# Decode loads and cache copies of a hybrid decoder layer issued from GpSimd's queue instead of SyncE's

## The chip, the cores and the metric

The kernel runs on one core of a Trainium2 chip. The metric is the time of one execution on the device in microseconds (us). The engines are TensorE (PE, with its weight loads as PEld), VectorE (DVE), ScalarE (ACT), GpSimd (POOL) and SyncE (SP); each works through its own instructions in order, and they meet at semaphores. SP does nothing here but issue DMAs. GpSimd computes a little and issues DMAs too. "SPq" and "POOLq" in the profile's rows are the DMA queues of these two.

## The reference

One decoder layer, for a prompt of 1024 tokens and eight samples of one token each that share its weights. The samples' attention to the memory and the two window caches are what the change touches.

```
z = x @ w_in                                  # split into xr, yr, q, k, v, xq and three gates
xc, conv_new = causal_conv(xr, conv_buf, conv_w, conv_b)     # conv_new: the last 3 rows of [conv_buf, xr]
hs, h_new = rg_lru(xc, h0, ...)
a_out = hs * gelu(yr)
s_out, wk_new, wv_new = swa_decode(q, k, v, win_k, win_v, sinks)   # wk_new = [win_k, k][-128:]
c_out = mem_attn(xq, mem_k, mem_v)            # softmax(xq . mem_k / 16) @ mem_v, 4 heads of 256, 256 rows
merged = sum(sigmoid(g_n + b_n) * (br_n @ w_branch[n]) for the three branches)
h = layer_norm(ALPHA * x + merged @ w_out)
h = layer_norm(ALPHA * h + (silu(gt) * up) @ w_down)
```

All inputs and outputs are float32; `mem_k` and `mem_v` hold 8 x 256 x 4 x 256 numbers each, the two window caches 8 x 128 x 256 each.

## The kernel before, in words

Every matrix product is done in three float32r products of a high and a low part: ACT casts the high part (`split`, L81), DVE subtracts the low one (L82), PE multiplies three times (L115 to L117, L300 to L302, L1178 to L1180). The big projections are done in units of two column tiles by a fast scheme of seven products, the quarters 0 to 6. A unit loads four halves of weights (`half_raw`, L92, tile `ur`) into six rotating buffers; quarters 1, 2, 4 and 5 are sums of them (L284, tile `us`), and three quarters are prepared ahead of PE.

The stages follow one another: the opening and the projection of z (`project`), memory attention and windows with the branch products as filling, the output projection, the gate-and-up products in units (`units`), and the down product. In the projection two side jobs are pumped along, a step every quarter or two: the recurrent branch `lru`, and for each head h the decode attention to the memory, `dec_mem(h)`. PE's accumulation banks are emptied by ACT (`p1s`, `p5s`, `u2s`, and `zb` at L1393) and DVE (`za`, `zb` at L327 to L332), and each bank has to be empty before PE writes it again.

`dec_mem(h)` writes the eight queries of the head to the memory outside, and for each pair of samples reads them back spread over all partitions (L809, tile `dcq`, two buffers). For each of the eight samples it loads 256 KB of keys (L811, tile `dck`, two buffers), and DVE forms two sums of products with them (L815, tile `dcj`). After a softmax the same is done with the probabilities (L833, `dcpb`) and the values (L835, `dcv`; L839, `dcw`). Over the four heads that is 32 loads of keys, 32 of values and 32 spread ones, all on SP's queue, between the projection's weight loads and the stores of its results.

In `lru`, GpSimd copies what has to be kept of the convolution's state: two rows of the samples' old state (L741, one copy for each of eight channel tiles m), the new row (L742) and the prompt's last three (L740). It also computes one step of the recurrence (L768, tile `tr`) and keeps the last state (L775, L776). GpSimd's queue further carries the loads of two thirds of branch a's rows (L136, tiles H) and of the down product's rows (L1253, `gl`).

In `units` the two window caches are copied from input to output, shifted by one row, 1016 KB each: at unit 6 keys (`o_swk`), at unit 12 values (`o_swv`), at L1226 on SP's queue, behind the last weight load issued so far. Results of a unit are stored from `ft` to `scr_f` by two stores on SP (L1204).

The order in which each engine takes its instructions is not the order of the code: a scheduler sets it by priorities and by its own estimates of when things will be ready. `issue_after(ins)` puts what its block issues behind `ins` on the engine of `ins`.

Of the kernel before, what the change touches and what calls it, by code (L numbers as in the profile page):

```python
# [10 lines left out]
F32 = mybir.dt.float32  # L11
# [7 lines left out]
P = 128  # L19
# [39 lines left out]
class Builder:  # L59
# [645 lines left out]
    def lru_setup(self):  # L705
        self.scv = self.cst.tile([P, KT, 3, NB], F32, name="scv")
        self.scvo = self.cst.tile([P, KT, 3, NB], F32, name="scvo")
        self.sh = self.cst.tile([P, KT, NB], F32, name="sh")
        self.sho = self.cst.tile([P, KT, NB], F32, name="sho")
        self.pconv = self.cst.tile([P, KT, 3], F32, name="pconv")  # L710
        self.pho = self.cst.tile([P, KT], F32, name="pho")

    def load_lru(self):
        self.nc.sync.dma_start(self.scv, self.io["scv"])
        self.nc.sync.dma_start(self.sh, self.io["sh"])

    def store_lru(self):
        nc, io = self.nc, self.io
# [5 lines left out]
    def lru(self, m, xr, yr):  # L724

        nc, io, vec = self.nc, self.io, self.vec
        col = lambda base: vec[:, base + m:base + m + 1]
        stt = nc.vector.scalar_tensor_tensor
        wr = self.z.tile([P, 256], F32, tag="wlr", name=f"wlr{m}", bufs=1)
        nc.sync.dma_start(wr, io["wlru"][m])  # L730
        cw = [col(V_CW + 8 * i) for i in range(4)]
        xc = self.zt(f"xc{m}")
        nc.scalar.activation(xc, xr, AF.Identity, bias=col(V_CB), scale=cw[3])
        buf = self.scv[:, m, :, :]
        for i in (2, 1, 0):
            d = 3 - i
            stt(xc[:, d:TP], xr[:, :TP - d], cw[i], xc[:, d:TP], op0=ALU.mult, op1=ALU.add)
            stt(xc[:, TP:T], buf[:, i, :], cw[i], xc[:, TP:T], op0=ALU.mult, op1=ALU.add)
            yield
        nc.gpsimd.tensor_copy(self.pconv[:, m, :], xr[:, TP - 3:TP])  # L740
        nc.gpsimd.tensor_copy(self.scvo[:, m, 0:2, :], buf[:, 1:3, :])  # L741
        nc.gpsimd.tensor_copy(self.scvo[:, m, 2, :], xr[:, TP:T])  # L742
        wgh, wgl = (self.z.tile([P, 256], F32R, tag=f"wg{e}", name=f"wg{e}{m}", bufs=1) for e in "hl")
        self.split(wgh, wgl, wr)
        a, ti = self.zt(f"tr{m}"), self.zt(f"ti{m}")
        for c, (t0, n) in enumerate(THIRDS):
            xch, xcl = (self.z.tile([P, n], F32R, tag=f"xc{e}", name=f"xc{e}{m}_{c}", bufs=1) for e in "hl")
            self.split(xch, xcl, xc[:, t0:t0 + n])
            yield
            for j, (dst, hb) in enumerate(((a, self.hba), (ti, self.hbx))):  # L750
                ps = self.bank("o", f"g{m}_{j}_{c}")[:, :n]
                self.mm3(ps, [((wgh[:, j * P:(j + 1) * P], wgl[:, j * P:(j + 1) * P]), (xch, xcl))])
                nc.scalar.activation(dst[:, t0:t0 + n], ps, AF.Tanh, bias=hb[:, m:m + 1], scale=0.5)
                yield

        sp2, sp4n = self.sp2[:, m:m + 1], self.sp4n[:, m:m + 1]
        stt(ti, ti, 1.0, xc, op0=ALU.add, op1=ALU.mult)
        th = self.zt(f"th{m}")
        nc.scalar.activation(th, a, AF.Tanh, bias=sp2, scale=sp2)
        yield  # L760
        nc.scalar.activation(a, a, AF.Exp, bias=sp4n, scale=sp4n)
        yield
        sq = self.zt(f"sq{m}")
        nc.scalar.activation(sq, th, AF.Sqrt)
        stt(th, a, 1.0, th, op0=ALU.add, op1=ALU.mult)
# [10 lines left out]
        nc.gpsimd.tensor_copy(self.sho[:, m, :], sq[:, TP:T])  # L776
# [23 lines left out]
    def dec_mem(self, h):  # L800
# [5 lines left out]
        for b in range(NB):  # L806
            if b % 2 == 0:
                qb = ph.tile([P, 512], F32, tag="dq", name=f"dcq{b}_{h}", bufs=2)
                nc.sync.dma_start(qb.rearrange("p (b d) -> p b d", b=2), qr[b:b + 2, :].partition_broadcast(P))  # L809
            kk = ph.tile([P, 512], F32, tag="dk", name=f"dck{b}_{h}", bufs=2)  # L810
            nc.sync.dma_start(kk.rearrange("p (t d) -> p t d", t=2),  # L811
                              io["cmk"][b, :, h * 256:(h + 1) * 256].rearrange("(t p) d -> p t d", p=P))
            for kt in range(2):
                junk = ph.tile([P, 256], F32, tag="dj", name=f"dcj{b}_{h}_{kt}", bufs=1)
                nc.vector.scalar_tensor_tensor(junk, kk[:, kt * 256:(kt + 1) * 256], 1.0,  # L815
                                               qb[:, (b % 2) * 256:(b % 2 + 1) * 256], op0=ALU.mult, op1=ALU.mult,
                                               accum_out=sc[:, kt, b:b + 1])
            yield
# [11 lines left out]
        for b in range(NB):  # L830
            if b % 2 == 0:
                pb = ph.tile([P, 512], F32, tag="dq", name=f"dcpb{b}_{h}", bufs=2)
                nc.sync.dma_start(pb.rearrange("p (b k) -> p b k", b=2), pd[b:b + 2, :].partition_broadcast(P))  # L833
            vv = ph.tile([P, 512], F32, tag="dk", name=f"dcv{b}_{h}", bufs=2)
            nc.sync.dma_start(vv.rearrange("p (f k) -> p f k", f=2),  # L835
                              io["cmvT"][b, h * 256:(h + 1) * 256, :].rearrange("(f p) k -> p f k", p=P))
            for f in range(2):
                junk = ph.tile([P, 256], F32, tag="dj", name=f"dcw{b}_{h}_{f}", bufs=1)
                nc.vector.scalar_tensor_tensor(junk, vv[:, f * 256:(f + 1) * 256], 1.0,  # L839
# [366 lines left out]
    def units(self):  # L1206
# [13 lines left out]
        for n, (f, i) in enumerate(todo):  # L1220
            if i == 1 and f + 1 < NF:
                load(f + 1)
            if (f, i) in ((6, 2), (12, 2)):
                name, cache = ("o_swk", "cwk") if f == 6 else ("o_swv", "cwv")
                with self.tc.issue_after(self.last_load):
                    self.nc.sync.dma_start(io[name][:, 0:P - 1, :], io[cache][:, 1:P, :])  # L1226
# [294 lines left out]
```

## Time and profile before

| | us |
|---|---|
| median of three runs | 1951.6 (1949.46 to 1952.06) |
| the profiled execution | 1951.06 |
| its span, first to last instruction | 1949.3 |
| mean granted TensorE clock | 0.997 |
| PE waits for other engines, 90 to 600 us | 3.3 |
| PE waits for other engines, 1300 to 1700 us | 2.3 |

The profile is of one execution. A row of the waits names the waiting engine, line and tile, then the engine, line and tile that ended the wait. A row of the timeline gives start, duration, engine, line, operation, output and inputs, and in square brackets how long the engine had been idle and what ended that. Rows with two times and a colon are stretches: length, then the busy time and number of instructions of PE, PEld, DVE, ACT and GpSimd, the granted clock, the share of the DMA engines and GB/s.

### The profile page before, as it was taken

How to read it: one execution, taken by the hardware profiler on the slowest of the kernel's cores; microseconds unless marked ns; L12 is line 12 of the kernel's file. 1: busy time of each engine (PE TensorE's matmuls, PEld its weight loads, DVE VectorE, ACT ScalarE, POOL GpSimd, SP SyncE). 2: the span in 40 equal slices, each digit the busy share in tenths (PEclk: the TensorE clock that was granted, in tenths of full speed). 3: DMA queues.
4: the chain of work that ended last, by engine and by line, in shares of the span. 5: the costliest groups of instructions: out<-in, count | busy, mean ns of one | idle time of the engine just before them, and what ended most of it. 6: DMA issues, size and time to landing. Idle time of an engine off the chain costs nothing. (4 is left out here: it accounts for less than half of the span.)

```text
span 1949.3 us, 37970 instructions
## 1 busy us (share of the span) xinstructions
PE 1912.5 (98%) x14356; PEld 1880.8 (96%) x14356; DVE 1364.0 (70%) x2875; ACT 1013.5 (52%) x2198; POOL 141.9 (7%) x218
## 2 busy tenths in 40 slices
PE   8999999999999999999999999999999999999997
PEld 8999999999999999989999999999999999999997
DVE  8678887888777555379877557976565665757566
ACT  5465565465556445378775245643333333635444
POOL 1000000000011200012210000000000000402002
PEclk9999999999999999999999999999999999999999
DMA  7444545365323866567534341122222222846554
GB/s 231 145 164 147 171 166 183 128 216 168 130 90 137 275 213 206 156 169 221 157 88 154 118 142 44 45 75 99 78 87 88 87 82 71 279 131 190 155 159 139
DMA packets 170919, 281.92 MB, mean 145 GB/s; under 512 B 20864, under 2 KB 85456, under 8 KB 170704
## 3 DMA queue, kind: packets, MB, share of 16 engines
q1 hardware_dynamic: 165840, 264.72, 43.0%
q0 software_dynamic: 4896, 14.78, 2.3%
q8 instruction: 112, 1.84, 0.4%
q14 instruction: 71, 0.58, 0.1%
HBM read 214.64 MB, written 66.85 MB: 144 GB/s over the span
## 5 line engine op out<-in xcount | busy, mean ns | idle before, releaser
L1246 PE MATMUL dl<-gh,wd_l 128*128 128x384 f32 (+1 forms) x528 | 167.4, 317 | 3.0 <-DVE wd_l L82 3.0
L1244 PE MATMUL dl<-gh,wd_h 128*128 128x384 f32 (+1 forms) x528 | 167.0, 317 | 1.0 <-ACT gh L81 1.0
L1245 PE MATMUL dl<-gl,wd_h 128*128 128x384 f32 (+1 forms) x528 | 167.2, 317 | 0.0
L1246 PEld LDWEIGHTS dl<-gh,wd_l 128*128 128x128 f32 x528 | 99.0, 188 | 3.5 <-DVE wd_l L82 3.5
L1244 PEld LDWEIGHTS dl<-gh,wd_h 128*128 128x128 f32 x528 | 98.9, 188 | 1.3 <-ACT gh L81 1.3
L1245 PEld LDWEIGHTS dl<-gl,wd_h 128*128 128x128 f32 x528 | 99.0, 188 | 0.5 <-DVE gl L82 0.5
L1253 POOL DMA_DIRECT2D gl<-scr_f x66 | 35.6, 540 | 789.0 <-PE fb L1179 630.8
L81 ACT CAST u_1h<-us 128x512 fp32r<-128x512 f32 x48 | 29.8, 621 | 87.6 <-issue 43.5
L592 ACT ACTIVATE bp<-bp,bst 128x257 f32<-128x257 f32 (+1 forms) x128 | 62.8, 493 | 18.0 <-DVE bst L588 17.7
L284 DVE TENSOR_TENSOR us<-ur,ur 128x512 f32<-128x512 f32 x96 | 66.0, 688 | 5.0 <-DMA ur<-win 2.9
L81 ACT CAST u_2h<-us 128x512 fp32r<-128x512 f32 x48 | 29.7, 619 | 76.5 <-PE fb L1179 38.2
L284 DVE TENSOR_TENSOR us<-us,ur 128x512 f32<-128x512 f32 x96 | 66.2, 689 | 2.3
L82 DVE TENSOR_TENSOR u_6l<-ur,u_6h 128x512 fp32r<-128x512 f32 x48 | 33.0, 688 | 43.8 <-PE fb L1180 28.5
L115 PE MATMUL brs<-bsH,wbs_h 128*128 128x384 f32 (+1 forms) x192 | 61.0, 319 | 1.0 <-ACT bsH L81 1.0
L82 DVE TENSOR_TENSOR u_4l<-us,u_4h 128x512 fp32r<-128x512 f32 x48 | 33.0, 687 | 40.1 <-PE fb L1180 29.1
L116 PE MATMUL brs<-bsL,wbs_h 128*128 128x384 f32 (+1 forms) x192 | 61.0, 318 | 0.0
L117 PE MATMUL brs<-bsH,wbs_l 128*128 128x384 f32 (+1 forms) x192 | 60.9, 317 | 0.0
L588 DVE CUSTOM_DVE_ANT_0 bp<-bs,mask,nsnk 128x256 f32<-128x256 f32 (+1 forms) x128 | 54.7, 458 | 3.3 <-PE bs L585 2.2
L82 DVE TENSOR_TENSOR u_5l<-us,u_5h 128x512 fp32r<-128x512 f32 x48 | 33.1, 690 | 30.0 <-PE fd L1180 14.6
L1198 ACT ACTIVATE ft<-za 128x516 f32<-128x516 f32 x40 | 25.5, 636 | 52.4 <-DVE za L1197 52.0
L81 ACT CAST u_5h<-us 128x512 fp32r<-128x512 f32 x48 | 30.0, 625 | 38.2 <-DVE us L284 24.7
L81 ACT CAST u_0h<-ur 128x512 fp32r<-128x512 f32 x48 | 29.8, 621 | 38.1 <-PE ub L301 19.2
(2019 smaller groups left out, 8112.7 us busy)
## 6 DMA issues: line engine op xcount, KB each, us to landing
ur<-win SPq DMA_DIRECT2D x112, 256.0 KB
ur<-wgu SPq DMA_DIRECT2D x80, 256.0 KB
scr_f<-ft SPq DMA_DIRECT2D x40, 258.0 KB
gl<-scr_f POOLq DMA_DIRECT2D x44, 192.0 KB, 4.8
dck<-cmk SPq DMA_DIRECT2D x32, 256.0 KB
dcv<-cmvT SPq DMA_DIRECT2D x32, 256.0 KB
st<-scr_q SPq DMA_DIRECT2D x32, 256.0 KB
scr_g<-za SPq DMA_DIRECT2D x10, 516.0 KB
```

The source lines that it names most:

```text
L81: ins = self.nc.scalar.copy(hi, src).ins
L82: self.nc.vector.tensor_sub(lo, src, hi.bitcast(F32))
L115: nc.tensor.matmul(ps, sh, mh, start=i == 0, stop=False)
L116: nc.tensor.matmul(ps, sh, ml, start=False, stop=False)
L117: self.last_mm = nc.tensor.matmul(ps, sl, mh, start=False, stop=closes and i == last).ins
L284: nc.vector.tensor_add(src, a, b)
L588: nc.vector.tensor_tensor_reduce(pg[g], s[:, u * 256:u * 256 + n], msk, 1.0, snk[:, g:g + 1], ALU.add, ALU.min, st[:, g:g + 1])
L592: nc.scalar.activation(x, x, AF.Exp, bias=st[:, g:g + 1], scale=-1.0, accum_out=st[:, 4 + g:5 + g])
L1244: nc.tensor.matmul(ps, sh, mh, start=k == 0, stop=False)
L1245: nc.tensor.matmul(ps, sh, ml, start=False, stop=False)
L1246: self.last_mm = nc.tensor.matmul(ps, sl, mh, start=False, stop=closes and k == NF - 1).ins
L1253: self.nc.gpsimd.dma_start(lo.bitcast(F32), self.scf[f][:, t0:t0 + n])
```

## The change

It does three things. The 96 loads of `dec_mem` go out from GpSimd's queue, the key loads behind GpSimd's copy of the convolution's old state. That copy is made once, for all eight channel tiles, right after the state is loaded. And the two cache copies go out from GpSimd's queue too, each behind a new tiny copy on GpSimd (`pace`) that reads the first `p1s` tile of its unit.

```diff
@@ load_lru
+        self.conv_kept = self.nc.gpsimd.tensor_copy(self.scvo[:, :, 0:2, :], self.scv[:, :, 1:3, :]).ins
@@ lru
         nc.gpsimd.tensor_copy(self.pconv[:, m, :], xr[:, TP - 3:TP])
-        nc.gpsimd.tensor_copy(self.scvo[:, m, 0:2, :], buf[:, 1:3, :])
         nc.gpsimd.tensor_copy(self.scvo[:, m, 2, :], xr[:, TP:T])
@@ dec_mem, keys
-                nc.sync.dma_start(qb.rearrange("p (b d) -> p b d", b=2), qr[b:b + 2, :].partition_broadcast(P))
+                nc.gpsimd.dma_start(qb.rearrange("p (b d) -> p b d", b=2), qr[b:b + 2, :].partition_broadcast(P))
             kk = ph.tile([P, 512], F32, tag="dk", name=f"dck{b}_{h}", bufs=2)
-            nc.sync.dma_start(kk.rearrange("p (t d) -> p t d", t=2),
-                              io["cmk"][b, :, h * 256:(h + 1) * 256].rearrange("(t p) d -> p t d", p=P))
+            with self.tc.issue_after(self.conv_kept):
+                nc.gpsimd.dma_start(kk.rearrange("p (t d) -> p t d", t=2),
+                                    io["cmk"][b, :, h * 256:(h + 1) * 256].rearrange("(t p) d -> p t d", p=P))
...
@@ dec_mem, values: the loads of pb and vv likewise from nc.sync to nc.gpsimd
...
@@ units
-                with self.tc.issue_after(self.last_load):
-                    self.nc.sync.dma_start(io[name][:, 0:P - 1, :], io[cache][:, 1:P, :])
+                with self.tc.issue_after(self.nc.gpsimd.tensor_copy(self.pace, st[f]["s", 0, 0][:, :1]).ins):
+                    self.nc.gpsimd.dma_start(io[name][:, 0:P - 1, :], io[cache][:, 1:P, :])
```

The scheduler's order changes with it. PE's order differs at two places only, the starts of units 8 and 14, where the two halves' first products were interleaved before and now stand one after the other.

On SP around the first cache copy (`ur` are the weight halves of one unit, `scr_f_85` to `scr_f_87` the results of units 5 to 7), before:

```order
L92 DMA ur_11_17775<-wgu 128x512
L1226 DMA o_swk<-cwk 8x2x16256
L1204 DMA scr_f_85<-ft_0_17613 256x1x258
L1204 DMA scr_f_85<-ft_1_17629 256x1x258
L1204 DMA scr_f_86<-ft_0_17866 256x1x258
L1204 DMA scr_f_86<-ft_1_17882 256x1x258
L92 DMA ur_00_18022<-wgu 128x512
L92 DMA ur_01_18024<-wgu 128x512
L92 DMA ur_10_18026<-wgu 128x512
L92 DMA ur_11_18028<-wgu 128x512
L1204 DMA scr_f_87<-ft_0_18118 256x1x258
L1204 DMA scr_f_87<-ft_1_18134 256x1x258
```

and with the change:

```order
L92 DMA ur_11_17769<-wgu 128x512
L1206 DMA scr_f_85<-ft_0_17607 256x1x258
L1206 DMA scr_f_85<-ft_1_17623 256x1x258
L92 DMA ur_00_18017<-wgu 128x512
L92 DMA ur_01_18019<-wgu 128x512
L92 DMA ur_10_18021<-wgu 128x512
L92 DMA ur_11_18023<-wgu 128x512
L1206 DMA scr_f_86<-ft_0_17861 256x1x258
L1206 DMA scr_f_86<-ft_1_17877 256x1x258
L92 DMA ur_00_18269<-wgu 128x512
L92 DMA ur_01_18271<-wgu 128x512
```

The copy is gone from SP, and each unit's two stores again alternate with the four loads of a later unit; before, the stores of `scr_f_85` and `scr_f_86` stood together ahead of the loads.

On ACT, where unit 8's first quarter is split (`u_0h`) and unit 7's gate is formed (`ft`), before:

```order
L1190 COPY u2s_0_18084<-fb_0_17992 128x258
L1190 COPY u2s_1_18098<-fb_1_18007 128x258
L1198 ACTIVATE ft_0_18118<-za_0_18117 128x516
L1198 ACTIVATE ft_1_18134<-za_1_18133 128x516
L81 CAST u_0h<-ur_00_18022 128x512
L81 CAST u_1h<-us_1_18168 128x512
L81 CAST u_2h<-us_2_18206 128x512
L81 CAST u_3h<-ur_01_18024 128x512
```

and with the change:

```order
L1192 COPY u2s_0_18079<-fb_0_17987 128x258
L81 CAST u_0h<-ur_00_18017 128x512
L1192 COPY u2s_1_18093<-fb_1_18002 128x258
L81 CAST u_1h<-us_1_18163 128x512
L81 CAST u_2h<-us_2_18201 128x512
L1200 ACTIVATE ft_0_18113<-za_0_18112 128x516
L81 CAST u_3h<-ur_01_18019 128x512
L1200 ACTIVATE ft_1_18129<-za_1_18128 128x516
```

The cast of `u_0h` stood behind both tanh of `ft` and now stands ahead of them.

On SP in the key loop of head 1 before (`dcq` the spread queries, `dck` the keys, one row per sample):

```order
L809 DMA dcq_1_2509<-dcq_2501 128x512
L809 DMA dcq_1_2689<-dcq_2501 128x512
L811 DMA dck_1_2691<-cmk 128x2x256
L92 DMA ur_01_2904<-win 128x512
L811 DMA dck_1_2771<-cmk 128x2x256
L809 DMA dcq_1_2857<-dcq_2501 128x512
L811 DMA dck_1_2859<-cmk 128x2x256
L92 DMA ur_10_2906<-win 128x512
L811 DMA dck_1_2948<-cmk 128x2x256
L809 DMA dcq_1_3027<-dcq_2501 128x512
```

and on GpSimd with the change:

```order
L742 COPY pconv<-za_2110 128x3
L743 COPY scvo<-za_2110 128x8
L813 DMA dck_1_2596<-cmk 128x2x256
L810 DMA dcq_1_2509<-dcq_2501 128x512
L810 DMA dcq_1_2689<-dcq_2501 128x512
L813 DMA dck_1_2691<-cmk 128x2x256
L813 DMA dck_1_2771<-cmk 128x2x256
L810 DMA dcq_1_2857<-dcq_2501 128x512
L813 DMA dck_1_2859<-cmk 128x2x256
L813 DMA dck_1_2948<-cmk 128x2x256
```

The same loads in the same order, without weight loads between them, behind GpSimd's own copies of the recurrent branch.

On DVE in the same loop (`dcj` the sums of products, `za` and `zb` the emptying of PE's banks, `u_6l` and `u_0l` weight splits), before:

```order
L815 SCALAR_TENSOR_TENSOR dcj_1_0_2773,dcs_2508<-dck_1_2771,dcq_1_2689 128x256
L815 SCALAR_TENSOR_TENSOR dcj_1_1_2775,dcs_2508<-dck_1_2771,dcq_1_2689 128x256
L327 TENSOR_TENSOR za_2701<-uc_1_2716,p1s_1_2589 128x258
L82 TENSOR_TENSOR u_0l<-ur_00_2602,u_0h 128x512
L815 SCALAR_TENSOR_TENSOR dcj_1_0_2861,dcs_2508<-dck_1_2859,dcq_1_2857 128x256
L815 SCALAR_TENSOR_TENSOR dcj_1_1_2863,dcs_2508<-dck_1_2859,dcq_1_2857 128x256
L329 SCALAR_TENSOR_TENSOR zb_2739<-ub_0_2561,p5s_0_2629 128x258
L815 SCALAR_TENSOR_TENSOR dcj_1_0_2950,dcs_2508<-dck_1_2948,dcq_1_2857 128x256
L815 SCALAR_TENSOR_TENSOR dcj_1_1_2952,dcs_2508<-dck_1_2948,dcq_1_2857 128x256
L329 SCALAR_TENSOR_TENSOR zb_2739<-ub_1_2576,p5s_1_2644 128x258
```

and with the change:

```order
L817 SCALAR_TENSOR_TENSOR dcj_1_0_2861,dcs_2508<-dck_1_2859,dcq_1_2857 128x256
L817 SCALAR_TENSOR_TENSOR dcj_1_1_2863,dcs_2508<-dck_1_2859,dcq_1_2857 128x256
L327 TENSOR_TENSOR za_2701<-uc_1_2716,p1s_1_2589 128x258
L82 TENSOR_TENSOR u_0l<-ur_00_2602,u_0h 128x512
L817 SCALAR_TENSOR_TENSOR dcj_1_0_2950,dcs_2508<-dck_1_2948,dcq_1_2857 128x256
L817 SCALAR_TENSOR_TENSOR dcj_1_1_2952,dcs_2508<-dck_1_2948,dcq_1_2857 128x256
L329 SCALAR_TENSOR_TENSOR zb_2739<-ub_0_2561,p5s_0_2629 128x258
L817 SCALAR_TENSOR_TENSOR dcj_1_0_3031,dcs_2508<-dck_1_3029,dcq_1_3027 128x256
L329 SCALAR_TENSOR_TENSOR zb_2739<-ub_1_2576,p5s_1_2644 128x258
L82 TENSOR_TENSOR u_1l<-us_1_2777,u_1h 128x512
```

The sums of the fifth and sixth sample stand closer together, and a first sum of the seventh (`dck_1_3029`) now stands ahead of the second `zb`; before, it came behind `za`, further down.

More of the change, by code (lines that the diff above doesn't have):

```diff
@@ L710, in lru_setup @@
         self.pconv = self.cst.tile([P, KT, 3], F32, name="pconv")
+        self.pace = self.cst.tile([P, 1], F32, name="pace")
         self.pho = self.cst.tile([P, KT], F32, name="pho")
@@ L832, in dec_mem @@
                 pb = ph.tile([P, 512], F32, tag="dq", name=f"dcpb{b}_{h}", bufs=2)
-                nc.sync.dma_start(pb.rearrange("p (b k) -> p b k", b=2), pd[b:b + 2, :].partition_broadcast(P))
+                nc.gpsimd.dma_start(pb.rearrange("p (b k) -> p b k", b=2), pd[b:b + 2, :].partition_broadcast(P))
             vv = ph.tile([P, 512], F32, tag="dk", name=f"dcv{b}_{h}", bufs=2)
-            nc.sync.dma_start(vv.rearrange("p (f k) -> p f k", f=2),
-                              io["cmvT"][b, h * 256:(h + 1) * 256, :].rearrange("(f p) k -> p f k", p=P))
+            nc.gpsimd.dma_start(vv.rearrange("p (f k) -> p f k", f=2),
+                                io["cmvT"][b, h * 256:(h + 1) * 256, :].rearrange("(f p) k -> p f k", p=P))
             for f in range(2):
```

## The prediction

> **What bounds the kernel now.** I read the page's first two parts, then PE's waits as a whole and by stage, then the stretches in which PE stood still, and last the queues of SP and GpSimd (POOL).
>
> ```profile
> span 1949.3 us, 37970 instructions
> PE 1912.5 (98%) x14356; PEld 1880.8 (96%) x14356; DVE 1364.0 (70%) x2875; ACT 1013.5 (52%) x2198; POOL 141.9 (7%) x218
> ```
>
> PE is busy for 98% of the span, so 1949.3 - 1912.5 = 36.8 us is all that any change of waits could ever return. The moved loads lie in the projection (about 30 to 470 us), the two cache copies in the unit stage (1354 and 1477 us). These are PE's waits between 90 and 600 us, and those between 1300 and 1700 us (line, tile, released by; us in total, times, longest):
>
> ```profile
> PE ub L300 <- ACT zb L1393: 2.0, 2, 1.4
> PE g L115 <- ACT tr L753: 0.5, 1, 0.5
> PE ub L300 <- DVE zb L329: 0.5, 1, 0.5
> PE vt L407 <- DVE v L419: 0.3, 1, 0.3
> ...
> PE fb L1180 <- DVE u_0l L82: 1.3, 2, 0.6
> ```
>
> That is 3.3 us in the projection and 1.3 us in the unit stage: 4.6 us in 1950, or 0.24%. A measurement of this kernel can tell about 0.2%, or 3.9 us, from no change. The ceiling of the gain is therefore just over what can be seen; a loss has no such ceiling.
>
> Why PE waits in the unit stage is seen on SP around the first copy (start, duration, line, DMA, count):
>
> ```profile
> 1337.18 1.19 SPq L1204 DMA_DIRECT2D scr_f<-ft  x2
> 1341.62 12.56 SPq L92 DMA_DIRECT2D ur<-wgu  x4
> 1354.23 0.86 SPq L1226 DMA_DIRECT2D o_swk<-cwk  x1
> 1357.30 21.30 SPq L1204 DMA_DIRECT2D scr_f<-ft  x4
> 1378.69 2.03 SPq L92 DMA_DIRECT2D ur<-wgu  x4
> ```
>
> The normal turn is two stores, then four weight loads. Behind the copy the stores of two units stand together, the second pair waits for its unit to end, and the next unit's loads are issued at 1378.7, some 17 us after their usual time of 1361.7 (1341.6 plus the 20 us of a unit). The order of the work on ACT was made for loads that late: the gate's two tanh stand ahead of u_0h.
>
> ```profile
> 1393.76 0.64 ACT L1198 ACTIVATE ft<-za 128x516 f32<-128x516 f32 x1 [7.33 <-DVE za L1197]
> 1395.74 0.60 ACT L81 CAST u_0h<-ur 128x512 fp32r<-128x512 f32 x1
> 1398.61 0.39 PE L1180 MATMUL fb<-H_0h,u_0l 128*128 128x258 f32 x1 [0.64 <-DVE u_0l L82]
> 1520.21 0.39 PE L1180 MATMUL fb<-H_0h,u_0l 128*128 128x258 f32 x1 [0.64 <-DVE u_0l L82]
> ```
>
> ACT sits idle for 7.3 us in front of a tanh while the loads have landed, u_0h and so u_0l come late, and PE waits 0.64 us; the same again behind the second copy.
>
> In the projection the worst wait is in the key loop of head 1. First DVE's rows, then those behind it:
>
> ```profile
> 187.12 0.43 DVE L815 SCALAR_TENSOR_TENSOR dcj<-dck,dcq 128x256 f32<-128x256 f32 x1 [2.34 <-DMA dcq<-dcq]
> 190.98 0.42 DVE L815 SCALAR_TENSOR_TENSOR dcj<-dck,dcq 128x256 f32<-128x256 f32 x1 [0.64 <-DMA dck<-cmk]
> 199.02 0.43 DVE L815 SCALAR_TENSOR_TENSOR dcj<-dck,dcq 128x256 f32<-128x256 f32 x1 [1.42 <-DMA dck<-cmk]
> 203.32 0.42 DVE L332 TENSOR_TENSOR za<-ud,u2s 128x258 f32<-128x258 f32 x1
> 203.77 0.21 ACT L1412 ACTIVATE qdc<-za 128x8 f32<-128x8 f32 x1 [2.45 <-DVE za L332]
> 204.84 0.37 ACT L1393 ACTIVATE zb<-ub 128x258 f32<-128x258 f32 x1
> 205.25 0.39 PE L300 MATMUL ub<-t01h,u_0h 128*128 128x258 f32 x1 [1.42 <-ACT zb L1393]
> ```
>
> DVE works in order, so its waits for the decode loads push back za, which ACT needs for qdc, behind which stands the zb that frees PE's bank. Here DVE's lateness goes straight into PE. Over the whole projection DVE waits so:
>
> ```profile
> DVE dcj L815 <- DMA dck<-cmk: 7.1, 10, 1.4
> DVE dcw L839 <- DMA dcv<-cmvT: 7.0, 7, 1.7
> DVE dcj L815 <- DMA dcq<-dcq: 4.8, 3, 2.3
> DVE dcw L839 <- DMA dcpb<-dcpd: 2.3, 4, 0.8
> ```
>
> 21.2 us of waits for decode loads cost PE at most its 3.3 us; the rest went into the time in which DVE would have waited for PE anyway.
>
> **The change, part by part.**
>
> *The two cache copies off SP.* In the new order SP's loads and stores keep their normal turn through both places, u_0h stands ahead of both tanh, and PE's two interleaved openings are straight. What is gained is the two waits of 0.64 us: -1.3. The count of matmuls in the stretch says it could be a little more: 36 against 44 in an undisturbed 5 us (the second row below), 8 x 5/44 = 0.9 us; twice that is 1.8, the other end.
>
> ```profile
> 1395.00:1400.00 5.00, 4.36 (x36) 4.15 (x36) 4.87 (x11) 1.77 (x4) 0.00 (x0) 1.00 0.32 105
> 1355.00:1360.00 5.00, 5.00 (x44) 5.00 (x44) 3.54 (x9) 1.63 (x3) 0.00 (x0) 1.00 0.96 319
> ```
>
> The copy itself keeps the DMA engines full for about 5 us (the last row: share 0.96). From GpSimd it starts when the new small copy `pace` has read the unit's first p1s, about 1.5 us into unit 6. Unit 8 starts near 1398 (PE's wait above), unit 6 two units of 20 us earlier, so that is near 1359; there the copy meets the first two weight loads of unit 8 at 1361.7. Those are needed by u_0h near 1386 (20 us after 1365.9, where unit 7's u_0h ran): 24 us of cover, so nothing. `pace` also gives p1s a second reader, on an engine with nothing else to do there: nothing.
>
> *One conv copy instead of eight.* GpSimd saves seven of eight copies, and now the first loads stand behind the one.
>
> ```profile
> 25.60 5.31 POOL L741 COPY scvo<-scv 128x16 f32<-128x16 f32 x8 [25.16 <-DMA scv<-scv]
> 30.50 1.03 SPq L811 DMA_DIRECT2D dck<-cmk  x2
> 83.81 0.42 DVE L815 SCALAR_TENSOR_TENSOR dcj<-dck,dcq 128x256 f32<-128x256 f32 x1 [2.04 <-DMA dcq<-dcq]
> ```
>
> The first two key loads go out at about 27 instead of 30.5 and are used at 83.8: nothing. GpSimd was idle before and after those copies: nothing.
>
> *The 96 decode loads from SP to GpSimd.* Three effects. First, the issue: 96 x 0.54 us = 52 us of GpSimd time in 440 us (twice that, 104, if a load of 256 short rows takes double the 128 rows of gl), on an engine that is 7% busy: no bound. What it holds up are GpSimd's own small steps (pconv, tr, pho, sho); I laid the times of these in the trace against the new order, and none of them stands ahead of a load that was issued earlier than it ran. Second, dcq no longer queues on SP behind stores and weight loads. Third, the time from issue to data, L, may grow, and two buffers per load mean that each pair of batches waits one L.
>
> ```profile
> 182.05 1.42 SPq L809 DMA_DIRECT2D dcq<-dcq  x2
> 188.05 0.38 SPq L811 DMA_DIRECT2D dck<-cmk  x1
> 194.18 0.38 SPq L811 DMA_DIRECT2D dck<-cmk  x1
> ...
> L1253 POOL DMA_DIRECT2D gl<-scr_f x66: 536/538/595, 1662.9 to 1856.4; - x66
> DMA to landing us min/median/max: 2.7/4.3/5.4
> ...
> DMA to landing us min/median/max: 2.6/3.7/4.8
> ```
>
> On SP, L was at most 187.12 - 182.05 = 5.1 us for dcq, 190.98 - 188.05 = 2.9 and 199.02 - 194.18 = 4.8 for dck; a middle of 3.8. From GpSimd no 256 KB load is in the trace; the nearest are gl (192 KB, beside full DMA engines: 2.7/4.3/5.4) and the H rows of the branch stage (192 KB: 2.6/3.7/4.8, the last row). They bound L by 2.6 and 5.4. I take 3.5: a little under the H rows' median because those are sixteen loads issued in a row, well above their minimum because the load is a third larger and has twice as many rows. The new order on DVE puts the pairs nearer together and one pair more ahead of za, so three rounds of L now stand between the first dcj and za. By DVE's rows and L = 3.5 za ends 17.7 us after the first dcj, against 203.32 + 0.34 - 187.12 = 16.5 before: +1.2. The first dcj comes when dcq lands: at 3.5 to 4.3 instead of 5.1 it is 0.8 to 1.6 earlier: -1.2. Sum for this loop: 0. The loop of head 0 is built alike (its PE wait is the other 0.6): 0. The other six loops cost PE 0.5 us at most, and their slack takes up a half us per round. Ends: both zb waits and the 0.5 gone, -2.5; L at 4.3, three rounds in two loops, 6 x 0.8 = +4.8.
>
> The Trainium skill (DMA: Bandwidth & Descriptors, section Latency and other measured facts) gives about 1 us to the first byte for GpSimd's DMAs and 0.6 for SP's. By that estimate L would be 2.9 + 0.4 = 3.3 in an idle machine and the sum 6 x 0.2 = 1.2 us lower than mine; the trace has no pair of equal loads from both queues, so I leave the sum at the rows.
>
> **Sum.** -1.3 (unit stage) + 0 (projection) + 0 (the rest) = -1.3: the profiled execution's 1951.06 (span 1949.3 and 1.8 around it) becomes 1949.8. The median of the three runs is 1951.6, 0.5 higher; on that scale it is 1950.3.
>
> **Rivals.**
>
> *B, the projection gains too.* If SP's queue was what made dcq and dck late, as 4.8 and 5.1 against 2.9 suggest, DVE's waits fall, and PE's waits on ub (2.5) and g (0.5) go with them: -1.8 - 3.0 = -4.8, 1946.8. Against it: the denser order on DVE, and that PE's waits were spread over four causes.
>
> *C, slower: the loads land later from GpSimd.* In the loops of heads 0 and 1 PE's wait follows DVE's one for one, over six rounds. From L = 3.5 + 1.3/6 = 3.7 it eats the gain of the unit stage; at 4.3, gl's median, it is +4.8 - 1.3 = +3.5, and with a half us from each of two other dense loops, +4.5: 1956. For it: the H rows' median is 3.7, and more than half of gl's loads took 4.3. Against it: those were issued one behind another, while here at most four are under way.
>
> *D, slower by far: GpSimd does not get its descriptors out beside a busy DVE.* The worst case in the trace is a tiny GpSimd copy that took 3.5 us instead of 0.2 beside a DVE scan:
>
> ```profile
> L776 POOL COPY sho<-sq x8: 191/394/3545, 152.5 to 618.5; 128x8 f32<-128x8 f32 x8
> L827 DVE TENSOR_SCALAR dcp<-dcp,dcst 8x256 f32<-8x256 f32 x4 | 1.3, 336 | 0.0
> ```
>
> If each of six rounds were held for 3.3 us more, that is +20, 1970. Against it: GpSimd's DMA issues took 595 ns at the longest. The Trainium skill (SBUF - State Buffer, section Who interferes with whom) says that GpSimd's descriptor writing is locked out only by DVE copies, casts and tensor_scalar in a two-port mode, not by tensor_tensor. By that rule D needs such instructions, and the last row shows the only ones between 80 and 470 us: four, 1.3 us in all.
>
> *E, it does nothing:* the copies still disturb PE from their new place, and the loads are hidden anyway: 1951.6.
>
> **How the numbers follow.** Forecast 0.58, B 0.17, C 0.17, D 0.03, E 0.05. The range goes from B's 1946.8 to just under C's 1956 and leaves out D and half of C. Faster by over 0.2% (under 1947.7) is most of B and a sliver of the forecast: 0.18. Slower (over 1955.5) is about two thirds of C, and D: 0.16. Within it: 0.66.
>
> **What would show it.** Right: no PE wait on u_0l after 1300 us; SP's stores and loads in their turn; PE's waits on zb in the first 250 us between 1 and 3.5 us; a landing time of dck between 3 and 4. Wrong: dck and dcv landing at over 4.2 us with PE waiting on zb more often (C), or DVE's waits for decode loads falling under 12 us and PE's zb waits gone (B); GpSimd issues of several us (D).

## The result, and the profile after

| kernel | median of the runs, us | lowest to highest |
|---|---|---|
| before, beside it | 1951.83 (4 runs) | 1949.46 to 1954.84 |
| changed | 1972.63 (4 runs) | 1965.50 to 1975.98 |

The ratio is 1.0111, with a 95% interval of 1.0093 to 1.0129: the change costs some 21 us. The forecast was 1950.3. The profiled execution of the changed kernel is the fastest of its four, 1965.5; the other three had a mean granted clock of 0.991 to 0.993 where this one has 0.995, and that difference is part of the story below.

First the page: the first part, then the DMA issues (KB each, median us from issue to landing).

```profile
span 1963.7 us, 38011 instructions
PE 1916.2 (98%) x14356; PEld 1884.7 (96%) x14356; DVE 1364.4 (69%) x2875; ACT 1013.4 (52%) x2198; POOL 195.9 (10%) x311
...
ur<-win SPq DMA_DIRECT2D x112, 256.0 KB, 3.3
...
dck<-cmk POOLq DMA_DIRECT2D x32, 256.0 KB, 3.8
dcv<-cmvT POOLq DMA_DIRECT2D x32, 256.0 KB, 3.4
```

PE's busy time grew by only 3.7 us, the span by 14.4. GpSimd is busy for 54 us more and far from a bound. The landings lie in the band that the prediction called right, between 3 and 4, and yet the kernel is slower. Where the time goes is seen in PE's waits between 90 and 600 us (us in total, times, longest):

```profile
PE ub L300 <- DVE zb L329: 8.2, 4, 3.2
PE ub L300 <- ACT zb L1395: 4.0, 3, 1.7
PE ub L300 <- ACT zb L1393: 2.4, 2, 2.0
PE g L116 <- DVE xcl L82: 1.3, 2, 0.7
PE g L115 <- ACT tr L754: 0.6, 1, 0.6
PE dct L823 <- ACT vd L409: 0.3, 1, 0.3
```

That is 16.8 us where it was 3.3, and 14.6 of it is PE waiting for a bank that zb has not yet freed. DVE's waits for the decode loads went from 21.2 to 37.0 us:

```profile
DVE dcj L817 <- DMA dck<-cmk: 17.8, 15, 2.0
DVE dcw L841 <- DMA dcv<-cmvT: 10.5, 10, 2.1
DVE dcj L817 <- DMA dcq<-dcq: 4.4, 3, 2.8
DVE dcw L841 <- DMA dcpb<-dcpd: 4.3, 3, 1.9
```

How the one becomes the other is seen in the value loop of head 0, where PE had waited for nothing before. DVE's rows in that stretch, before and then after, are cut to the waits for loads, a weight split (`u_5l`) as a mark of how far DVE has come, and what stands nearest to zb (`ge` and the scan belong to the recurrent branch):

```profile
131.37 0.43 DVE L839 SCALAR_TENSOR_TENSOR dcw<-dcv,dcpb 128x256 f32<-128x256 f32 x1 [0.56 <-DMA dcpb<-dcpd]
...
146.45 0.69 DVE L82 TENSOR_TENSOR u_5l<-us,u_5h 128x512 fp32r<-128x512 f32 x1
...
149.41 2.28 DVE L772 TENSOR_TENSOR_SCAN sq<-tr,ti 128x1024 f32<-128x1024 f32 x1
...
154.56 0.41 DVE L329 SCALAR_TENSOR_TENSOR zb<-ub,p5s 128x258 f32<-128x258 f32 x1
154.90 1.22 DVE L781 SCALAR_TENSOR_TENSOR ge<-ge,zb 128x1032 f32<-128x1032 f32 x1
```

```profile
132.69 0.43 DVE L841 SCALAR_TENSOR_TENSOR dcw<-dcv,dcpb 128x256 f32<-128x256 f32 x1 [1.16 <-DMA dcpb<-dcpd]
...
138.06 0.42 DVE L841 SCALAR_TENSOR_TENSOR dcw<-dcv,dcpb 128x256 f32<-128x256 f32 x1 [0.55 <-DMA dcv<-cmvT]
...
144.33 0.42 DVE L841 SCALAR_TENSOR_TENSOR dcw<-dcv,dcpb 128x256 f32<-128x256 f32 x1 [1.17 <-DMA dcv<-cmvT]
...
149.66 0.69 DVE L82 TENSOR_TENSOR u_5l<-us,u_5h 128x512 fp32r<-128x512 f32 x1
...
156.23 1.23 DVE L782 SCALAR_TENSOR_TENSOR ge<-ge,zb 128x1032 f32<-128x1032 f32 x1
157.38 2.28 DVE L773 TENSOR_TENSOR_SCAN sq<-tr,ti 128x1024 f32<-128x1024 f32 x1
...
159.64 0.42 DVE L329 SCALAR_TENSOR_TENSOR zb<-ub,p5s 128x258 f32<-128x258 f32 x1
```

The first zb comes 5.1 us later than before, and two things add up in that. DVE lost 0.56 us to decode loads before and 2.88 us after; these 2.3 us are most of the 3.2 us by which u_5l is late. Apart from its waits for the loads DVE has no gap of note in this stretch, in either kernel, so it never gets the time back before the next zb. The other 1.9 us come behind u_5l and are the new order: it puts two more sums (0.7 us) and one `ge` (1.2 us), which stood behind this zb before, ahead of it. PE's row behind it, and then the clock (per stretch: length, busy time of PE, PEld, DVE, ACT and GpSimd with counts, granted clock, DMA share, GB/s):

```profile
160.11 0.39 PE L300 MATMUL ub<-ts60h,u_6h 128*128 128x258 f32 x1 [3.17 <-DVE zb L329]
```

```profile
156.00:160.00 4.00, 0.94 (x8) 0.74 (x7) 4.00 (x6) 2.09 (x3) 0.70 (x2) 1.00 0.77 239
...
160.30:163.70 3.40, 3.40 (x17) 3.40 (x17) 3.40 (x7) 0.79 (x1) 0.85 (x2) 0.51 0.02 5
163.70:167.00 3.30, 3.30 (x30) 3.30 (x29) 3.30 (x5) 2.01 (x5) 2.76 (x2) 0.99 0.40 163
```

PE stood for 3.17 us, and then ran 17 matmuls in 3.4 us where the next 3.3 us hold 30: the granted clock was 0.5. So this wait cost 3.2 us and then 1.7 more. The trace has four such stretches before 800 us, at 160, 208, 430 and 672; before the change there was one, at 656.

The two copies did what was forecast. PE's waits between 1300 and 1700 us, then SP and GpSimd around the first copy:

```profile
PE dl L1246 <- ACT gh L81: 1.0, 1, 1.0
```

```profile
1356.40 12.61 SPq L92 DMA_DIRECT2D ur<-wgu  x4
1372.11 1.19 SPq L1206 DMA_DIRECT2D scr_f<-ft  x2
1376.58 12.61 SPq L92 DMA_DIRECT2D ur<-wgu  x4
```

```profile
1374.39 0.65 POOL L1228 DMA_DIRECT2D o_swk<-cwk  x1 [0.15 <-issue]
```

The two waits on u_0l are gone, SP's turn is two stores, four loads, every 20 us, and the copy goes out 2.2 us ahead of the weight loads (2.7 in the forecast).

The profiled execution's ledger: PE's waits between 60 and 640 us +13.5 (16.8 against 3.3), three more stretches at half clock 3 x 1.7 = +5.1, unit stage -1.3, other waits of PE between 640 and 1300 us -1.8 (7.2 against 9.0). Together +15.5, against 14.4 measured.

### The profile page after: what moved, and what is told of

It reads as the page before. It is cut to its first block, busy times and chain, and to the rows that moved or that the text cites. A ratio compares the mean times of both kernels' runs of the same rounds, so it can differ in the third digit from the quotient of the medians.

```text
span 1963.7 us, 38011 instructions
## 1 busy us (share of the span) xinstructions
PE 1916.2 (98%) x14356; PEld 1884.7 (96%) x14356; DVE 1364.4 (69%) x2875; ACT 1013.4 (52%) x2198; POOL 195.9 (10%) x311
## 5 line engine op out<-in xcount | busy, mean ns | idle before, releaser
L81 ACT CAST u_1h<-us 128x512 fp32r<-128x512 f32 x48 | 29.8, 620 | 84.9 <-issue 47.8
L81 ACT CAST u_0h<-ur 128x512 fp32r<-128x512 f32 x48 | 29.8, 621 | 40.5 <-PE ub L301 19.8
L81 ACT CAST u_4h<-us 128x512 fp32r<-128x512 f32 x48 | 29.7, 619 | 34.0 <-PE fb L1181 23.0
```

What stands on the lines that cost most here:

```text
L81: ins = self.nc.scalar.copy(hi, src).ins
```

## The experiments

Two theories at first. **L, lateness:** the data come later from GpSimd, and two buffers don't cover it. **O, order:** the scheduler, which expects loads from GpSimd to be early, put DVE's sums nearer together and one pair more ahead of za and zb, and that lets PE run dry. The second can be told apart cleanly: the program gives DVE, ACT and PE the same instructions before and after, so one kernel's order can be laid on the other. All ratios are to the kernel before, run beside on the same chip (its medians there were 1950.75, 1951.35, 1950.77 and 1951.11).

**1. The loads on GpSimd in the old order, and on SP in the new one.** The edit is the same in both: at the end of the build the rows of the projection on DVE, ACT and PE get edges of issue order (no waits), from a table of the other kernel's order.

```
+        for name, ranks in _ORDER.items():
+            rows = [i for i in self.nc.cur_bb.bb.instructions if i.engine == getattr(mybir.EngineType, name)]
+            for p, q in zip(ranks, ranks[1:]):
+                self.tc.add_manual_dep(rows[q], rows[p].name, mybir.DependencyInfo(
+                    mybir.DependencyClass.NoSync, mybir.DependencyReason.DATA), reason="hold_order")
```

> The changed kernel with one thing put back: DVE's, ACT's and PE's rows of the projection stand in the order of the kernel before; the loads stay on GpSimd. Theory L (the data simply come later from GpSimd: 0.72 us of issue and 3.8 us, up to 6.8, of landing, with two buffers): DVE still waits some 35 us for decode loads, PE some 12 to 17 us in the projection, three or four dips of the granted clock, 1962 to 1973. Theory O (the new order, with the sums nearer together and one pair more ahead of za and zb, is what lets PE run dry): DVE's waits fall toward 21 us, PE waits 3 to 6 us in the projection, one dip, 1949 to 1953. If both share it, 1955 to 1960.

Measured: 1.0080 (1.0066 to 1.0094), 1965.87; DVE waits 33.0 us for the four decode loads, PE 12.6 in the projection, and the clock stands at half four times 3.4 us. That is L's case.

> The kernel before (all loads and copies on SP) with one thing taken over: the order of DVE's, ACT's and PE's rows in the projection is that of the changed kernel. Theory L (landing from GpSimd): no loads from there, so PE's waits in the projection stay at 3 to 6 us and the time at 1951 to 1955. Theory O (the order): PE waits 12 us or more in the projection, two or three dips of the clock more, 1962 to 1970.

Measured: 1.0018 (1.0009 to 1.0027), 1952.68; PE waits 6.8 us (3 to 6, it was said), one stretch at half clock. The new order alone costs 3.5 us, the loads in the old order 15.6, both together some 21. O is real and the smaller part. At the wait of 3.17 us shown above, both have a share. The loads alone and the order alone, PE's rows:

```profile
159.15 0.39 PE L349 MATMUL ub<-ts60h,u_6h 128*128 128x258 f32 x1 [1.25 <-DVE zb L378]
```

```profile
157.69 0.39 PE L349 MATMUL ub<-ts60h,u_6h 128*128 128x258 f32 x1 [1.37 <-DVE zb L378]
```

**2. The copies alone.** The edit: the two copies of the diff, with `pace`, in the kernel before.

> The kernel before with the two cache copies alone on GpSimd, behind the small copy; the loads stay on SP, and the order of DVE, ACT and PE in the projection is untouched. Both theories: the two waits of PE on u_0l go, -1.3 us by the waits, 1950.3 where the kernel before has 1951.6; the projection has its 3.3 us of PE waits and one dip of the clock. A third view (the copies disturb the unit stage from their new place): 1952 to 1956.

Measured: 0.9997 (0.9988 to 1.0006), 1949.5. The trace has no wait on u_0l. The time agrees with -1.3 us and can't tell it from nothing; that it gains is shown by the waits alone. PE's waits in the projection were to stay at 3.3 us with one stretch at half clock; the profiled execution (span 1953.4) has 5.5 us and three, though no load moved. So two us of PE's waits, read from one execution each, tell no two kernels apart.

**3. A third buffer for the key and value loads.** The room comes from the sums' products, which nobody reads, and from the probabilities' tile:

```
-            kk = ph.tile([P, 512], F32, tag="dk", name=f"dck{b}_{h}", bufs=2)
+            kk = ph.tile([P, 512], F32, tag="dk", name=f"dck{b}_{h}", bufs=3)
...
-                junk = ph.tile([P, 256], F32, tag="dj", name=f"dcj{b}_{h}_{kt}", bufs=1)
-                nc.vector.scalar_tensor_tensor(junk, kk[:, kt * 256:(kt + 1) * 256], 1.0,
+                nc.vector.scalar_tensor_tensor(kk[:, kt * 256:(kt + 1) * 256], kk[:, kt * 256:(kt + 1) * 256], 1.0,
...
-        pr = ph.tile([NB, 256], F32, tag="dp", name=f"dcp{h}", bufs=1)
+        pr = self.sm.tile([NB, 256], F32, tag="drow", name=f"dcp{h}", bufs=1)
```

> The changed kernel, order of DVE, ACT and PE held as it is there, with three buffers instead of two for the key and value loads (the sums' unused products are written over their input and the probabilities take the place of another small tile, to make the room). Theory L: a third load is under way while two are summed, so about 5 us more cover for each; DVE's waits for dck and dcv fall from 30 us to under 10, PE's waits in the projection from 17 to under 6, 1949 to 1955. Theory O: the sums still stand as dense ahead of za and zb, so most of PE's waits stay, 1960 to 1972.

Measured: 1.0012 (1.0002 to 1.0021), 1952.61. With the changed kernel's own order and its loads on GpSimd, a third buffer takes back nine tenths of the loss. DVE's waits for dck and dcv fall from 28.3 to 10.3 us (to "under 10", it was said), PE's from 16.8 to 6.1 (to "under 6"). What remains, 0.0012, is about what the order cost in experiment 1. No run has the products written over their input and two buffers; a sum takes the same time either way (418 ns at the median in the kernel before, 416 to 418 with three buffers and loads on SP).

**4. Which loads.** Within L the loads can differ: theory R blames the rounds of the key and value loads, theory S the spread loads that start each loop. One kind goes back to SP, in the order of the kernel before, the copies on GpSimd; the edit for the first kernel:

```
-                nc.gpsimd.dma_start(qb.rearrange("p (b d) -> p b d", b=2), qr[b:b + 2, :].partition_broadcast(P))
+                nc.sync.dma_start(qb.rearrange("p (b d) -> p b d", b=2), qr[b:b + 2, :].partition_broadcast(P))
...
-                nc.gpsimd.dma_start(pb.rearrange("p (b k) -> p b k", b=2), pd[b:b + 2, :].partition_broadcast(P))
+                nc.sync.dma_start(pb.rearrange("p (b k) -> p b k", b=2), pd[b:b + 2, :].partition_broadcast(P))
```

> Loads split: the 64 key and value loads (dck, dcv) and the two copies on GpSimd, the 32 spread loads (dcq, dcpb) back on SP; DVE, ACT and PE in the order of the kernel before. Two theories within 'the data come later'. Theory R (the round of two buffers: from the last read of a buffer to the next data in it GpSimd adds a pause of 0.38 us before it issues, where SP issues within 0.1, and about 0.3 to landing; some 30 rounds wait): it needs only these loads, so nearly all of the loss of the run with all loads there and this order (1.0080) is here: 1.006 to 1.009, 1961 to 1968. Theory S (the spread loads, which start each loop, land late: 4.1 to 4.4 us at the median): 0.999 to 1.002.

Measured: 1.0107 (1.0093 to 1.0121), 1972.52: on R's side, and worse than R's range. Its waits of PE between 60 and 480 us:

```profile
PE ub L349 <- DVE zb L378: 7.2, 4, 4.3
PE ub L349 <- ACT zb L1455: 5.9, 2, 4.1
PE g L165 <- DVE xcl L131: 2.1, 1, 2.1
PE ub L349 <- ACT zb L1453: 2.0, 2, 1.2
PE g L164 <- ACT tr L803: 0.6, 1, 0.6
```

The key and value loads alone give the whole loss. What DVE's waits add up to does not tell it: they are 24.7 us in all here, less than the 33.0 with all loads on GpSimd, and PE waits 20.0 between 60 and 640 us.

> The reverse split: the 32 spread loads and the two copies on GpSimd, the 64 key and value loads on SP; order of DVE, ACT and PE as in the kernel before. Theory R: two spread buffers hold four batches, so the pause is met four times less; DVE waits 20 to 25 us for decode loads, PE 3 to 6 us in the projection: 0.999 to 1.002, 1949 to 1954. Theory S: 1.005 to 1.008.

Measured: 1.0036 (1.0024 to 1.0047), 1958.11; DVE waits 29.8 us, PE 8.3. Neither theory had this: the spread loads cost too, if a third as much. The two halves add up to 1.0143 and together they are 1.0080, so they are not separate terms; why the key and value loads alone cost more than all loads together is not settled. (In that trace they also land later, 4.1 and 3.9 us at the median against 3.8 and 3.6 with all loads on GpSimd.)

**5. Lateness by itself, without GpSimd's queue.** All loads stay on SP, in the old order; each key and value load waits for a small memset on GpSimd, of one column or of all 512.

```
             kk = ph.tile([P, 512], F32, tag="dk", name=f"dck{b}_{h}", bufs=2)
+            nc.gpsimd.memset(kk[:, :1], 0.0)
             nc.sync.dma_start(kk.rearrange("p (t d) -> p t d", t=2),
...
             vv = ph.tile([P, 512], F32, tag="dk", name=f"dcv{b}_{h}", bufs=2)
+            nc.gpsimd.memset(vv[:, :1], 0.0)
             nc.sync.dma_start(vv.rearrange("p (f k) -> p f k", f=2),
```

> The lateness by itself, without GpSimd's queue: the kernel before, all loads and copies on SP, DVE, ACT and PE in its order, but each key and value load waits for a GpSimd memset of one column of its buffer, which itself waits for the buffer's last read. SP then issues some 0.3 to 0.6 us later in every round (the memset's 0.1 us and two hand-overs; GpSimd's own loads in the changed kernel issue 0.38 after the last read). Theory R (lateness per round is what costs, wherever it comes from): DVE's waits for dck and dcv rise from 14 us to 20 to 30, PE's waits in the projection from 3.3 to 8 to 14, one or two more dips of the clock, 1.003 to 1.009. If it is GpSimd's queue itself (its transfers being slower on the way, or in the way of others) that costs: 0.999 to 1.002.

Measured: 1.0037 (1.0023 to 1.0050), 1957.53, on R's side: DVE waits 21.2 us for dck and dcv, PE 8.2, one more stretch at half clock.

> The same with a memset of the whole buffer (128x512), some 0.4 to 0.6 us longer, so that a round is about 1 us later than in the kernel before. Theory R: clearly slower than with the one column: 1.008 to 1.020, PE's waits in the projection 12 to 25 us, three to six more dips. Queue theory: 0.999 to 1.004.

Measured: 1.0093 (1.0075 to 1.0111), 1969.77, on a queue that is not GpSimd's. PE waits 14.0 us, as R has it; the profiled execution, 1963.7, has one more stretch at half clock and not three to six. Of its runs, those with a mean clock of 0.996, 0.995 and 0.992 took 1963.7, 1965.8 and 1971.8: the spread between runs goes with the clock. The memsets did not act by another way that the traces show: DVE's sums take 418 ns at the median as before, and the waits for weight loads, which stand behind the held loads on SP, are 2.6 us on DVE before, 2.1 (and 0.6 on ACT) with the short memset and 3.0 with the long one.

The size of the lateness can be read in one place in all these kernels, the first round in the key loop of head 1: from the end of the last read of a buffer (an accumulator read) to the issue of the next load into it, and to the sum that waits for that load. Before, DVE's row; SP's issue at 188.05 and the sum at 190.98 stand in the prediction:

```profile
187.94 0.08 DVE L815 DVE_READ_ACCUMULATOR dcj<-dck,dcq 128x1 f32 x1
```

All loads on GpSimd in the old order, GpSimd's row and DVE's two:

```profile
192.42 0.71 POOL L862 DMA_DIRECT2D dck<-cmk  x1 [5.79 <-DVE dcj L866]
```

```profile
191.94 0.08 DVE L866 DVE_READ_ACCUMULATOR dcj<-dck,dcq 128x1 f32 x1
...
195.59 0.43 DVE L866 SCALAR_TENSOR_TENSOR dcj<-dck,dcq 128x256 f32<-128x256 f32 x1 [1.25 <-DMA dck<-cmk]
```

The long memset, the rows of GpSimd, SP and DVE:

```profile
192.03 0.53 POOL L860 MEMSET dck<- 128x512 f32 x1 [18.73 <-DVE dcj L865]
```

```profile
192.59 0.38 SPq L861 DMA_DIRECT2D dck<-cmk  x1
```

```profile
191.84 0.08 DVE L865 DVE_READ_ACCUMULATOR dcj<-dck,dcq 128x1 f32 x1
...
195.53 0.42 DVE L865 SCALAR_TENSOR_TENSOR dcj<-dck,dcq 128x256 f32<-128x256 f32 x1 [1.28 <-DMA dck<-cmk]
```

| kernel, order as before, two buffers | last read to issue, us | to data, us | more than before | ratio |
|---|---|---|---|---|
| before (SP) | 0.03 | 2.96 | | 1 |
| spread loads on GpSimd | 0.02 | 2.94 | 0 | 1.0036 |
| SP behind the short memset | 0.24 | 3.24 | 0.28 | 1.0037 |
| all loads on GpSimd | 0.40 | 3.57 | 0.61 | 1.0080 |
| key and value loads on GpSimd | 0.41 | 3.61 | 0.65 | 1.0107 |
| SP behind the long memset | 0.67 | 3.61 | 0.65 | 1.0093 |

The pause ahead of the issue is much the same in every round in which a sum waits for its load (0.03, 0.24, 0.41 and 0.66 us at the median for SP, the short memset, GpSimd and the long one); the time from issue to data is not, it runs from 2.8 to 4.8 us in the kernel before, and this round is one of its short ones. A quarter of a us more per round cost 7 us, some 0.6 cost 16 to 21, whichever queue they come from. That is theory R: what counts is the length of the round of two buffers. GpSimd adds to it twice: some 0.4 us between the last read and its issue, where SP needs next to nothing, and then 3.17 instead of 2.93 us from issue to data, its issue itself lasting 0.71 instead of 0.38. The Trainium skill (DMA: Bandwidth & Descriptors, section Latency and other measured facts) gives GpSimd's DMAs 0.4 us more to the first byte. This round shows 0.24 us more from issue to data, and 0.6 in all with the pause ahead of the issue. (The spread loads' cost does not pass through this round: their first load lands later, issue to sum 5.5 against 5.1 us in the same loop.)

**6. Three buffers in the order of the kernel before**, with the loads on one queue or the other; the edits are those above, put together.

> All loads and both copies on GpSimd, three buffers for the key and value loads, and the order of the kernel before on DVE, ACT and PE. Theory R: the third buffer covers the pause (with the changed kernel's own order it gave 1.0012), and the looser order takes off another 0.002 to 0.003, what it took off with two buffers: 0.998 to 1.000, 1947 to 1951. If the order only mattered where loads were late: 1.001.

Measured: 0.9998 (0.9990 to 1.0007), 1950.62. All loads from GpSimd at no loss against the kernel before, as R has it.

> Loads on SP as before, copies alone on GpSimd (0.9997), and three buffers for the key and value loads, order of the kernel before: may beat both. DVE's 14 us of waits for dck and dcv go; PE's waits in the projection fall from 3.3 us to about 1.5; SP's queue is no longer held by an issue that waits for a buffer. 0.9975 to 0.9995, 1946 to 1950. If the two cache copies' 1.3 us and the projection's 3.3 are all that was ever to be had, not under 0.9975.

Measured: 0.9975 (0.9966 to 0.9985), 1945.57: it beats both kernels. DVE's waits for dck and dcv fell from 14 to 7.2 us, not to nothing. All of PE's waits between 60 and 480 us:

```profile
PE dct L870 <- ACT vd L458: 0.5, 1, 0.5
PE vt L456 <- DVE v L468: 0.3, 1, 0.3
PE g L164 <- ACT tr L803: 0.3, 1, 0.3
```

No bank is waited for any more.

> Key and value loads and both copies on GpSimd, spread loads on SP (the split that gave 1.0107), now with three buffers for the key and value loads; order of DVE, ACT and PE as in the kernel before. Theory R (the round of two buffers was 0.7 us longer from GpSimd, and a third buffer covers it): the loss goes whole, and it ends near the same kernel with these loads on SP (0.9975): 0.9965 to 0.999. Theory Q (GpSimd's transfers of these loads hold up others, whatever the buffers): 1.001 or more. What is left between 0.9998 (all loads on GpSimd, three buffers) and 0.9975 is then the spread loads' part.

Measured: 0.9984 (0.9974 to 0.9994), 1948.12. The split that cost 1.0107 with two buffers now gains; theory Q falls.

> The reverse split with three buffers: spread loads and copies on GpSimd, key and value loads on SP. Theory R: the key and value loads are covered on either queue, so what the spread loads cost from GpSimd (two buffers, each for two batches, the first of each loop on the path; 0.0039 with two key and value buffers) stays: 0.999 to 1.001, near the 0.9998 of all loads on GpSimd. If the spread loads cost only where the key and value loads were late too: 0.9965 to 0.9985.

Measured: 0.9974 (0.9964 to 0.9984), 1946.69, on the side of the last sentence: the spread loads, too, cost only while the key and value loads had no cover. It is level with the kernel that has all loads on SP, so moving loads to GpSimd gains nothing that can be seen; the third buffer does. One thing stays open: with three buffers either kind of load can go to GpSimd without a loss that can be told, but both together (0.9998) are 0.0023 behind all loads on SP, and these two intervals do not overlap. No run shows why.

All profiled executions beside each other: PE's waits between 60 and 640 us, and how many times 3.4 us the granted clock stood at 0.5 before 800 us (a stretch of 6.8 us counts as two).

| kernel | PE's waits | half clock | span | ratio of the runs |
|---|---|---|---|---|
| before | 3.3 | 1 | 1949.3 | 1 |
| changed | 16.8 | 4 | 1963.7 | 1.0111 |
| loads on GpSimd, old order | 12.6 | 4 | 1962.0 | 1.0080 |
| loads on SP, new order | 6.8 | 1 | 1952.7 | 1.0018 |
| copies alone on GpSimd | 5.5 | 3 | 1953.4 | 0.9997 |
| GpSimd, three buffers, new order | 6.1 | 4 | 1953.9 | 1.0012 |
| key and value loads on GpSimd | 20.0 | 7 | 1970.8 | 1.0107 |
| spread loads on GpSimd | 8.3 | 3 | 1958.6 | 1.0036 |
| SP, short memset | 8.2 | 2 | 1953.3 | 1.0037 |
| SP, long memset | 14.0 | 2 | 1961.9 | 1.0093 |
| GpSimd, three buffers, old order | 5.0 | 1 | 1950.4 | 0.9998 |
| SP, three buffers | 1.1 | 1 | 1941.9 | 0.9975 |
| key and value loads on GpSimd, three buffers | 3.0 | 1 | 1945.1 | 0.9984 |
| spread loads on GpSimd, three buffers | 1.9 | 0 | 1942.7 | 0.9974 |

## Why the prediction was wrong

- **Unit stage, -1.3: right.** Both waits on u_0l vanished, the copies cost nothing in their new place, and the mechanism was the one told.
- **Conv copy and GpSimd's issue time: right.** The one copy took 0.37 us and the first loads left at 25.6. The 96 issues took 64.4 us (64 of 0.72, 32 of 0.56), inside the 52 to 104, and bounded nothing.
- **L = 3.5, and "the first dcj 0.8 to 1.6 earlier": wrong, and the pause ahead of the issue was left out.** L was the time from issue to data. In the round measured above it is 3.17 us from GpSimd, and over the 25 rounds of the changed kernel in which a sum waits for its load it is 4.0 at the median; that 3.5 is close to the 3.57 of the whole round, pause and all, is luck. The size was weighed against "a middle of 3.8" for SP, which is the middle of two unlike rows of dck (2.9 and 4.8). Like with like, in the same round, SP needs 2.96 from the last read to data, so the move is +0.6 per round and not -0.3. And the first dcj of that loop came 5.3 us after the issue of dcq where it was 5.1: later, not earlier. Together the two errors made 0 of a loss: in the key loop of head 1 za ends 19.2 us after the first dcj, against 16.5 before and 17.7 in the forecast.
- **The step that failed: "the other six loops cost PE 0.5 us at most, and their slack takes up a half us per round".** It put 0 there. The key loops of heads 0 and 1 on which the sum was built grew only from 2.0 to 4.2 us of PE's waits. Most of the rest of the 16.8 us lies in those other loops: 3.17 at 160 (shown above), 2.04 at 258, 2.86 at 428, 1.75 at 482, and some smaller ones. That DVE waited there without harm showed that some slack was left, not how much; and the lateness of several rounds adds up before the next zb, as the value loop of head 0 shows with 2.88 us of waits in place of 0.56. The new order was weighed for the two key loops alone; in that value loop it set another 1.9 us of work ahead of zb.
- **A term that was missing: the clock.** Three more stretches at half clock, 5.1 us in the profiled execution. The others have a mean clock lower by 0.002 to 0.004; one such stretch takes 3.41 x 0.5 / 1964 = 0.0009 off the mean, so that is two to five more of 1.7 us, more than half of the 6 to 10 us by which they are longer.
- **The rivals.** What happened is C's mechanism, "the loads land later", at more than four times its price: C counted heads 0 and 1 and a half us from two other loops. B's reading (SP's queue was what made the loads late) is wrong: off that queue DVE's waits rose. D's starved descriptors did not occur: no issue of the moved loads took over 0.89 us. (Before, the longest issue of GpSimd was not the 595 ns of gl but the 735 ns of one H row, which changes nothing.) The sign that was to tell C, a landing over 4.2, was badly chosen: landing counts from the issue, and more than half of the lateness lies ahead of it. So the sign of being right, a landing of dck between 3 and 4, came true in a kernel that is slower. The sign that did tell was PE's waits on zb in the first 250 us, 7.3 us where 1 to 3.5 were to be.

## What to carry to other kernels

Before loads change queues, measure the whole round in one place for each: from the last read of the buffer to the issue, and on to the first use; the landing time alone leaves out the pause before the issue. An engine that waits for loads many times without harm has a slack of unknown size: multiply the lateness per round by the number of rounds that already wait, and take the product as a first estimate of the loss until something in the profile bounds it. In the kernel before, 17 sums wait for dck or dcv; 17 x 0.28 = 5, 17 x 0.61 = 10 and 17 x 0.65 = 11 us stand against 7, 16 and 18 measured (short memset, all loads on GpSimd, long memset), so here the product was some two thirds of the loss. Where two buffers wait for each load, a third buffer is the change to try first: here it gained 5 us with the loads where they were, and left 0.0023 between the queues where two buffers had left 0.0080.

## What the hardware showed that was not expected

Short waits of PE are followed by the half clock. In the traces of the kernels here, PE's waits in the projection (60 to 590 us) of 1.2 us or more fall out so: of 14 under 1.7 us none was followed by a stretch of 3.4 us at a granted clock of 0.5; of 18 between 1.7 and 2.5 us, 10 were, within 2 us; of the four above (2.86, 3.17, 4.05 and 4.27), all were, and no stretch in the projection came without such a wait. (Three of the stretches began up to 1 us before the wait ended.) The one with the wait of 4.27 us, in the kernel with the key and value loads on GpSimd, lasted 6.8 us:

```profile
432.00:435.40 3.40, 3.39 (x15) 3.39 (x16) 3.40 (x10) 1.49 (x4) 0.77 (x1) 0.50 0.00 0
435.40:438.80 3.40, 3.40 (x21) 3.40 (x21) 3.16 (x7) 0.81 (x3) 1.73 (x2) 0.64 0.60 233
```

Behind the projection even less was enough. Between 645 and 678 us each of the 14 traces has a wait of about 0.96 us and, 2 to 3.5 us later, one of 1.0 to 2.2; in 13 of them the half clock comes with the second wait, and the one without has the shortest, 1.03 us. It may be that waits that stand close together count together; no run tests it.

The Trainium skill (TensorE: Matmul & The Clock Gate, Part 1) lets the clock fall after an idle window of about 3.4 us; here waits of 1.8 us sufficed at times, which the runs show and do not explain. So a wait of PE of 2 us in the projection cost 2 or 3.7, and each of the four above 2.5 us cost 1.5 to 2.9 more (half of what was left of the stretch when the wait ended).
